# Four 32-row tiles for the samples' state update, rounded halves for the heads' sums, and another order of rows in the output projection

## The chip, the core and the metric

The kernel runs on one core of a Trainium2 chip. The metric is the device time of one execution in microseconds (us); less is better. The version before takes 2548.17 us, the median of three runs (2547.49 to 2548.25).

## What is computed

One decoder layer for 256 prompt tokens and 8 samples of 8 tokens, 320 tokens in all, with a model width of 2048. In the order of the reference:

```python
x = x + 0.5 * swiglu_ffn(rmsnorm(x, n_f1), f1_g, f1_u, f1_d)
m, s_new, buf_new = mixer(rmsnorm(x, n_mix), ...)        # w_in, heads and convolutions, w_out
x = x + m
x = x + cross_attn(rmsnorm(x, n_xa), mk, mv, xa_q, xa_o)
x = x + 0.5 * swiglu_ffn(rmsnorm(x, n_f2), f2_g, f2_u, f2_d)
y = rmsnorm_final(x)
```

The change lies in the mixer. One projection `w_in` feeds eight HGRN2 heads (group A) and a convolution of 31 taps over 1024 channels with a layer norm (group B); `w_out` maps their 2048 outputs back. A head keeps a 128 x 128 state per sequence. For each of the eight samples it computes

```python
S = exp(b_end)[..., None] * S + jnp.einsum('nhse,nhsd->nhed', k_to_end, vc)
o = rmsnorm(o, gnorm) * jax.nn.silu(zg)
```

with a sum over the sample's eight tokens in the first line (`k_to_end` is named `ket`, the tokens' values `vt`), and a mean over the head's 128 channels in the second.

## The kernel before

**Layout.** Activations lie with features on the 128 partitions and the 320 tokens along the free axis, so that the 2048 features are 16 tiles of 128 x 320. Weights come from memory in units of 128 x 1024 fp32 (eight blocks of 128 x 128). Each unit is split (lines 122 to 124) into a rounded high half `whi` in the type fp32r, cast by ScalarE (ACT), and the rest `wlo`, subtracted by VectorE (DVE). A block product (`mm3`, lines 188 to 195) is three fp32r matmuls into one PSUM bank: high by high, high by low, low by high. Matmuls on plain fp32 operands are used for the small products; the profile shows each of them as two instructions (transposes as one).

**PSUM.** Eight banks, in two sets of four: `acc` holds the sums of the projections, `sm` everything small.

**Mixer, input side.** `mixer_order` alternates convolutions and heads: c0, c1, h0, c2, h1, ... c7, h6, h7. A convolution takes two strips of `w_in` (16 blocks each), a head four (f, q, i, g in `head_in`). What follows a strip is not issued at once, but comes from two lists of generators: `hq` holds the heads' work (`head`, lines 639 to 764) and `cq` the convolutions' (`conv_taps`, 35 steps each, then `conv_norm`, 18 steps). After every fourth block product `pump` advances `hq` by one step and `cq` by CRATE = 1.65 steps on average. A step ends at a `yield`. So the order of the program interleaves projection and small work; within this order a scheduler places an instruction earlier or later when its operands are ready earlier or later.

**A head's steps.** Two empty ones; seven levels of a doubling scheme (lines 648 to 674, each a product of k and q into an `sm` bank, then DVE work on `qk` and a masked copy), with an empty step behind each, except in head 7; then transposes of k to tokens (`ket`) and of v (`vt`, `to_tokens`, lines 631 to 637: three transposes, one bank, one ACT copy); `vm`, eight copies of the last 64 tokens' values, each with the rows of one sample kept by the mask `vmask` (lines 687 and 688); the samples' read of the old state (line 695); the sums `po` (lines 707 and 710, a bank held to the head's end); the scaling of the eight states by ACT (line 717) and the prompt's chunk states (lines 723 to 730); the chunks' reads (line 710); the square `o2`; and then, in one step, lines 743 to 759:

```python
for b in range(2):                       # four samples each, 32 rows
    nc.tensor.matmul(ps, ket[rows, 2, :], vm[rows, 4 * b : 4 * b + 4, :]..., tile_position=(64 + 32 * b, 0))
    nc.vector.tensor_tensor(so, so, ps, ALU.add)
nc.tensor.matmul(ps[:, :T], ones, o2, start=True, stop=True)
root(o2, ps[:, :T], P)
```

`root` (lines 207 to 215) is square root, reciprocal and a correction step on ACT and DVE, with a scratch bank of `sm`. The last step scales, multiplies by the gate and splits the result into the pair `oc[h]`.

**Mixer, output side.** After the last strip, `while cq["jobs"]: pump()` empties the convolutions' list with no block products between. Then `w_out` is applied in two parts of 16 output tiles by 8 input tiles, part 0 with the convolutions' rows (8 to 15), part 1 with the heads' (0 to 7); `tick` goes on pumping, and `drain` empties both lists between the parts. Each output tile's sum lies in an `acc` bank until a DVE add to `x` (line 790).

Of the kernel before, what the change touches and what calls it, by code (L numbers as in the profile page):

```python
# [10 lines left out]
F32 = mybir.dt.float32  # L11
F32R = mybir.dt.float32r
U8 = mybir.dt.uint8
AF = mybir.ActivationFunctionType
ALU = mybir.AluOpType
AX = mybir.AxisListType

P = 128
DM = 2048
KT = DM // P  # L20
FF = 5632
FT = FF // P
NP = 256
NS = 64
T = NP + NS
# [26 lines left out]

CRATE = 1.65

# [7 lines left out]
def restride(ap, offset, dims):  # L62
    base = ap.ap
    return dataclasses.replace(ap, offset=ap.offset + offset, ap=[list(base[0])] + [list(d) for d in dims])


def hymba(tc, A, O):
# [3 lines left out]
    def tl(pool, shape, dt, tag, bufs):  # L71
        count[0] += 1
        return pool.tile(shape, dt, tag=tag, name=f"{tag}_{count[0]}", bufs=bufs)
# [9 lines left out]
    with (  # L83
# [11 lines left out]
        def sm():  # L95
            return tl(pp, [P, 512], F32, "sm", 4)
# [10 lines left out]
        msk = cp.tile([P, len(LEVELS), T], U8, name="msk")  # L107
        vmask = cp.tile([P, NSEQ], F32, name="vmask")
        sel = cp.tile([P, NS], F32, name="sel")
# [43 lines left out]
        def unit():  # L153
            while len(units) < 2 * G_TOT and len(units) < upos[0] + ahead[0]:
                fetch()
            u = units[upos[0]]
            units[upos[0]] = None
            upos[0] += 1
            return u
# [338 lines left out]
        with phase("mixer") as wk:  # L498

            def tmp(tag, bufs=2, w=T):  # L500
                return tl(wk, [P, w], F32, tag, bufs)

            qpad = wk.tile([P, NSEQ, 32], F32, name="qpad")
            nc.gpsimd.memset(qpad, 0.0)
            dws = [None] * NC
            csum = []
# [94 lines left out]
            def head_in(h):  # L601
                s0 = tl(wk, [P, NSEQ, P], F32, "t4", 4)
                nc.sync.dma_start(s0, A["s0"][h])
# [26 lines left out]

            def to_tokens(src, tag, bufs):
                ps = sm()
                for b, t0 in enumerate((0, P, T - P)):
                    nc.tensor.transpose(ps[:, b * P : (b + 1) * P], src[:, t0 : t0 + P], ident)
                out = tl(wk, [P, 3, P], F32, tag, bufs)
                nc.scalar.copy(out.rearrange("p a b -> p (a b)"), ps[:, : 3 * P])
                return out

            def head(h, s0, f, qk, late):
# [41 lines left out]
                )  # L681
                ket = to_tokens(k, "ket", 2)
                yield
                vt = to_tokens(late["v"], "vt", 2)
                up = slice(64, P)
                vm = tl(wk, [P, NSEQ, P], F32, "t4", 4)
                for i in range(NSEQ):
                    nc.scalar.activation(vm[up, i, :], vt[up, 2, :], AF.Copy, scale=vmask[up, i : i + 1])
                yield
# [50 lines left out]
                nc.scalar.activation(o2, po[:, :T], AF.Square)  # L740
                yield

                for b in range(2):
                    rows = slice(64 + 32 * b, 96 + 32 * b)
                    ps = sm()
                    nc.tensor.matmul(  # L746
                        ps,
                        ket[rows, 2, :],
                        vm[rows, 4 * b : 4 * b + 4, :].rearrange("p a b -> p (a b)"),
                        start=True,  # L750
                        stop=True,
                        tile_position=(64 + 32 * b, 0),
                    )
                    so = s0[:, 4 * b : 4 * b + 4, :].rearrange("p a b -> p (a b)")
                    nc.vector.tensor_tensor(so, so, ps, ALU.add)
                nc.sync.dma_start(O["ss"][h], s0)
                ps = sm()
                nc.tensor.matmul(ps[:, :T], ones, o2, start=True, stop=True)
                root(o2, ps[:, :T], P)
# [9 lines left out]
            for kind, i in mixer_order():  # L769
# [4 lines left out]
                else:  # L774
                    head_in(i)
            while cq["jobs"]:
                pump()


            stat = Stat(True)  # L780
            xg = []
            for part in range(2):
                if part:
                    drain()
                for n in range(KT):
                    ps = acc()
                    w = unit()
                    for kk in range(8):
                        mm3(ps[:, :T], w, kk, *oc[(1 - part) * NH + kk], kk == 0, kk == 7)
                    nc.vector.tensor_tensor(xs[n], ps[:, :T], xs[n], ALU.add)  # L790
                    if part:
                        xg.append(scaled_split(n, "xattn"))
                        stat.add(xs[n])
# [205 lines left out]
def pack(i):  # L999
# [9 lines left out]
    wout = strips(f["w_out"][0])  # L1009
    for half in (wout[:, :, 1024:], wout[:, :, :1024]):  # L1010
        groups.append(half.reshape(8, 2, P, 1024).transpose(0, 2, 1, 3).reshape(8, P, 2048))
    groups.append(strips(f["xattn_wq"][0]))
# [27 lines left out]
    for t0 in (0, P, NP):  # L1040
# [4 lines left out]
        for j, (H, wd) in enumerate(LEVELS):  # L1045
# [6 lines left out]
            msk[:, j, t0 : t0 + n] = m  # L1052
    vmask = np.zeros((P, NSEQ), np.float32)
    for j in range(NSEQ):
        vmask[64 + j * TS : 64 + (j + 1) * TS, j] = 1.0
    sel = np.zeros((P, NS), np.float32)
# [54 lines left out]
```

## Time and profile before

| | |
|---|---|
| median of three runs | 2548.17 us |
| the profiled execution's own time | 2546.1 us |
| its span, first to last instruction | 2544.3 us |
| TensorE clock granted | 0.998 of full speed |
| PE busy (matmuls) | 2521.4 us, 99% |
| DVE busy | 1482.4 us, 58% |
| ACT busy | 1047.3 us, 41% |
| DMA | 393.18 MB, mean 155 GB/s |

The profile is one execution. Engines: PE is TensorE's matmuls, PEld its weight loads, DVE is VectorE, ACT is ScalarE, POOL is GpSimd. L746 is line 746. In a timeline row stand the start in us from the span's start, the duration (of a run of rows: from the first start to the last end), engine, line, operation, the tiles written and read, and the count; what stands in brackets is how long the engine had been idle and what released it. Matmuls are pipelined, so that a row's duration is longer than the distance to the next row's start; it is the starts that tell the cost. The strips of `w_in` run from 984.9 to 1387.7 us, and part 0 of `w_out` follows.

### The profile page before, as it was taken

What the parts mean: (1) busy time and instruction counts of PE and PEld (TensorE: products, weight loads), DVE (VectorE), ACT (ScalarE), POOL (GpSimd) and SP (SyncE); (2) the same over time, 40 slices, a digit from 0 to 9 for tenths busy, and PEclk for the clock granted to TensorE, in tenths of its full rate; (3) what the DMA queues carried; (4) which work ended last, traced back from release to release, by engine and by line L of the source; (5) the groups of instructions that cost most, each with busy time, mean ns of one, the idle gap of its engine ahead of it and who ended that gap; (6) DMA issues with size and microseconds to landing.
All of it is one profiled execution on the core that took longest, in us unless ns stands there. A gap on an engine that the chain in (4) does not pass through costs nothing.

```text
span 2544.3 us, 41630 instructions
## 1 busy us (share of the span) xinstructions
PE 2521.4 (99%) x17300; PEld 2485.8 (98%) x17300; DVE 1482.4 (58%) x2115; ACT 1047.3 (41%) x1447; POOL 77.6 (3%) x88
## 2 busy tenths in 40 slices
PE   9999999999999999999999999999999999999997
PEld 9999999999999999999999999999999999999997
DVE  7555444444444567899888676644444444444444
ACT  6433333333333355555557455433333333333334
POOL 0100000000000020000000021100000000000002
PEclk9999999999999999999999999999999999999999
DMA  6544444444444446444443454444444444444443
GB/s 225 196 149 150 150 149 149 149 149 150 150 150 151 150 153 209 153 155 150 141 148 129 146 207 164 149 150 149 151 151 150 150 151 150 150 149 150 149 149 108
DMA packets 111357, 393.18 MB, mean 155 GB/s; under 512 B 12608, under 2 KB 16704, under 8 KB 111168
## 3 DMA queue, kind: packets, MB, share of 16 engines
q1 hardware_dynamic: 111024, 390.35, 45.5%
q8 instruction: 136, 2.23, 0.4%
q14 instruction: 53, 0.43, 0.0%
q10 hardware_dynamic: 144, 0.16, 0.0%
HBM read 380.71 MB, written 9.76 MB: 153 GB/s over the span
## 4 chain that ended last, share of the span: by engine, by line
PE 95%; DVE 2%; DMA 1%; ACT 1%; issue 1%; SPq 0%; POOLq 0%; DVEq 0%; ACTq 0%
PE acc L192 30%; PE acc L194 30%; PE acc L193 30%; PE sm L651 1%; DVE wlo L124 1%; PE acc L480 1%; PE acc L479 1%; PE acc L478 1%; DVE xgl L248 0%; PE sm L710 0%; ACT whi L123 0%; PE sm L746 0%; DMA t4k<-in_msk 0%; DMA mem<-in_mem 0%; DMA x<-in_x 0%
## 5 line engine op out<-in xcount | busy, mean ns | idle before, releaser
L123 ACT CAST whi<-raw 128x1024 fp32r<-128x1024 f32 (+1 forms) x692 | 722.2, 1045 | 1377.3 <-PE acc L193 981.5
L124 DVE TENSOR_TENSOR wlo<-raw,whi 128x1024 fp32r<-128x1024 f32 (+1 forms) x692 | 845.0, 1222 | 532.9 <-ACT whi L123 530.9
L192 PE MATMUL acc<-xgh,whi 128*128 128x320 f32 x3616 | 1128.4, 312 | 0.8 <-ACT whi L123 0.5
L194 PE MATMUL acc<-xgh,wlo 128*128 128x320 f32 x3616 | 1118.4, 309 | 1.0 <-DVE wlo L124 1.0
L193 PE MATMUL acc<-xgl,whi 128*128 128x320 f32 x3616 | 1117.7, 309 | 0.5 <-DVE xgl L248 0.4
L192 PEld LDWEIGHTS acc<-xgh,whi 128*128 128x128 f32 x3616 | 679.1, 188 | 4.6 <-issue 2.2
L193 PEld LDWEIGHTS acc<-xgl,whi 128*128 128x128 f32 x3616 | 679.1, 188 | 1.9 <-DVE xgl L248 1.0
L194 PEld LDWEIGHTS acc<-xgh,wlo 128*128 128x128 f32 x3616 | 678.7, 188 | 2.0 <-DVE wlo L124 1.7
L192 PE MATMUL acc<-hh,whi 128*128 128x320 f32 x1728 | 535.2, 310 | 2.1 <-ACT hh L123 2.0
L193 PE MATMUL acc<-hl,whi 128*128 128x320 f32 x1728 | 534.7, 310 | 1.5 <-DVE hl L124 1.5
L194 PE MATMUL acc<-hh,wlo 128*128 128x320 f32 x1728 | 534.1, 309 | 0.0
L192 PEld LDWEIGHTS acc<-hh,whi 128*128 128x128 f32 x1728 | 324.1, 188 | 4.2 <-ACT hh L123 2.8
L193 PEld LDWEIGHTS acc<-hl,whi 128*128 128x128 f32 x1728 | 324.4, 188 | 2.7 <-DVE hl L124 2.0
L194 PEld LDWEIGHTS acc<-hh,wlo 128*128 128x128 f32 x1728 | 324.4, 188 | 0.3 <-issue 0.2
L297 DVE SCALAR_TENSOR_TENSOR x<-acc,x 128x320 f32<-128x320 f32 x192 | 94.0, 490 | 228.2 <-PE acc L194 228.1
L230 POOL TENSOR_TENSOR ssq<-ssq,sq 128x320 f32<-128x320 f32 x57 | 62.1, 1089 | 1848.9 <-ACT sq L228 947.0
L550 DVE SCALAR_TENSOR_TENSOR hl<-u,vec,hl 128x256 f32<-128x256 f32 x240 | 112.3, 477 | 1.6
L262 DVE TENSOR_TENSOR fb<-acc,fa 128x320 f32<-128x320 f32 x87 | 42.7, 490 | 106.3 <-PE acc L194 106.2
L254 DVE TENSOR_TENSOR fa<-acc,r 128x320 f32<-128x320 f32 x87 | 42.7, 490 | 104.9 <-PE acc L194 104.9
L124 DVE TENSOR_TENSOR hl<-fb,hh 128x320 fp32r<-128x320 f32 x88 | 44.7, 509 | 0.0
L256 DVE TENSOR_TENSOR fa<-fa,r 128x320 f32<-128x320 f32 x88 | 42.5, 484 | 1.0 <-ACT fa L255 1.0
L255 ACT ACTIVATE fa<-fa 128x320 f32<-128x320 f32 x88 | 40.9, 465 | 4.2 <-DVE fa L254 4.2
(213 smaller groups left out, 1058.8 us busy)
## 6 DMA issues: line engine op xcount, KB each, us to landing
raw<-in_w SPq DMA_DIRECT2D x687, 512.0 KB, 3.6
t<-in_s SPq DMA_DIRECT2D x8, 512.0 KB, 5.0
out_ss<-t SPq DMA_DIRECT2D x8, 512.0 KB, 4.1
kv<-in_ck SPq DMA_DIRECT2D x8, 512.0 KB, 5.6
kv<-in_cv SPq DMA_DIRECT2D x8, 512.0 KB, 5.6
mem<-in_mem SPq DMA_DIRECT2D x4, 512.0 KB, 6.4
out_conv<-u SPq DMA_DIRECT2D x8, 167.0 KB, 3.5
x<-in_x SPq DMA_DIRECT2D x2, 640.0 KB, 7.3
```

Source lines behind the costliest of these rows:

```text
L123: nc.scalar.copy(hi, src)
L124: nc.vector.tensor_tensor(lo, src, hi.bitcast(F32), ALU.subtract)
L192: nc.tensor.matmul(out, hi, xh, start=first, stop=False)
L193: nc.tensor.matmul(out, hi, xl, start=False, stop=False)
L194: nc.tensor.matmul(out, lo, xh, start=False, stop=last)
L230: nc.gpsimd.tensor_tensor(self.total, self.total, s, ALU.add)
L254: nc.vector.tensor_tensor(t, pg[:, :T], r, ALU.mult)
L255: nc.scalar.activation(t, t, AF.Silu)
L256: nc.vector.tensor_tensor(t, t, r, ALU.mult)
L262: nc.vector.tensor_tensor(h, pu[:, :T], t, ALU.mult)
L297: nc.vector.scalar_tensor_tensor(xs[n], ps[:, :T], 0.5, xs[n], ALU.mult, ALU.add)
L550: nc.vector.scalar_tensor_tensor(dw[:, :NP], u[:, j : j + NP], cw, dw[:, :NP], ALU.mult, ALU.add)
```

## The change

Four edits.

1. The samples' state update. The sample tokens of k and v are spread so that each quarter of 32 partitions holds the 16 tokens of two samples (`spread` into the zeroed `kpad` and `vpad`, one ACT copy each). k's third transpose reads `kpad`; v gets a fourth transpose, of `vpad`. `vm` is then two full copies in place of eight half ones. The update is four products of 32 rows by 256 columns, at the tile positions (0, 0), (32, 0), (64, 0) and (96, 0), into four banks (three `sm`, one `acc`), followed by four DVE adds of 256 columns in place of two of 512.
2. The head's sum of squares. `o2` is split into two fp32r halves, `oh` (ACT) and `ol` (DVE), and summed by two fp32r matmuls with `ones_r` in place of one fp32 matmul. The sum and `root` move one step (one `yield`) behind the state update.
3. The order in `w_out`. Part 0 takes the rows of heads 0 to 6, part 1 the convolutions' and then head 7's; the weights are packed in memory to match, with the same bytes. Ahead of part 0 the loop now empties the heads' list down to its last entry, and the convolutions' list goes on in part 0.
4. CRATE is 1.5. The tag of `s0` and `vm` had four buffers; `s0` has three, `vm` one of its own.

```diff
--- before.py
+++ after.py
@@ -50,7 +50,10 @@
 
 G_TOT = 2 * 3 * FT + 8 + 48 + 16 + 4 + 4
 
-CRATE = 1.65
+CRATE = 1.5
+
+
+OUTPARTS = [list(range(7)), list(range(8, 16)) + [7]]
 
 
 def mixer_order():
@@ -105,7 +108,7 @@
         ident = cp.tile([P, P], F32, name="ident")
         eps = cp.tile([P, 1], F32, name="eps")
         msk = cp.tile([P, len(LEVELS), T], U8, name="msk")
-        vmask = cp.tile([P, NSEQ], F32, name="vmask")
+        vmask = cp.tile([P, 2], F32, name="vmask")
         sel = cp.tile([P, NS], F32, name="sel")
         at = [cp.tile([P, T], F32, name=f"at{i}") for i in range(2)]
         lb = cp.tile([P, NH], F32, name="lb")
@@ -500,8 +503,14 @@
             def tmp(tag, bufs=2, w=T):
                 return tl(wk, [P, w], F32, tag, bufs)
 
+            ones_r = wk.tile([P, P], F32R, name="ones_r")
+            nc.scalar.copy(ones_r, ones)
             qpad = wk.tile([P, NSEQ, 32], F32, name="qpad")
             nc.gpsimd.memset(qpad, 0.0)
+            kpad = wk.tile([P, P], F32, name="kpad")
+            nc.gpsimd.memset(kpad, 0.0)
+            vpad = wk.tile([P, P], F32, name="vpad")
+            nc.gpsimd.memset(vpad, 0.0)
             dws = [None] * NC
             csum = []
             oc = [None] * KT
@@ -599,7 +608,7 @@
                     yield
 
             def head_in(h):
-                s0 = tl(wk, [P, NSEQ, P], F32, "t4", 4)
+                s0 = tl(wk, [P, NSEQ, P], F32, "t4", 3)
                 nc.sync.dma_start(s0, A["s0"][h])
                 pf = acc()
                 strip(xg, pf[:, :T])
@@ -628,12 +637,17 @@
                 nc.scalar.activation(gt, pg[:, :T], AF.Silu)
                 late["g"] = gt
 
-            def to_tokens(src, tag, bufs):
+
+            def spread(dst, src):
+                nc.scalar.copy(restride(dst, 0, [[32, 4], [1, 16]]), restride(src, 0, [[16, 4], [1, 16]]))
+
+            def to_tokens(srcs, tag, bufs):
                 ps = sm()
-                for b, t0 in enumerate((0, P, T - P)):
-                    nc.tensor.transpose(ps[:, b * P : (b + 1) * P], src[:, t0 : t0 + P], ident)
-                out = tl(wk, [P, 3, P], F32, tag, bufs)
-                nc.scalar.copy(out.rearrange("p a b -> p (a b)"), ps[:, : 3 * P])
+                n = len(srcs)
+                for b, src in enumerate(srcs):
+                    nc.tensor.transpose(ps[:, b * P : (b + 1) * P], src, ident)
+                out = tl(wk, [P, n, P], F32, tag, bufs)
+                nc.scalar.copy(out.rearrange("p a b -> p (a b)"), ps[:, : n * P])
                 return out
 
             def head(h, s0, f, qk, late):
@@ -679,13 +693,15 @@
                     restride(qpad.rearrange("p a b -> p (a b)"), 0, [[64, 4], [40, 2], [1, TS]]),
                     restride(q, NP, [[2 * TS, 4], [TS, 2], [1, TS]]),
                 )
-                ket = to_tokens(k, "ket", 2)
-                yield
-                vt = to_tokens(late["v"], "vt", 2)
-                up = slice(64, P)
-                vm = tl(wk, [P, NSEQ, P], F32, "t4", 4)
-                for i in range(NSEQ):
-                    nc.scalar.activation(vm[up, i, :], vt[up, 2, :], AF.Copy, scale=vmask[up, i : i + 1])
+                spread(kpad, k[:, NP:])
+                ket = to_tokens((k[:, :P], k[:, P:NP], kpad), "ket", 2)
+                yield
+                v = late["v"]
+                spread(vpad, v[:, NP:])
+                vt = to_tokens((v[:, :P], v[:, P:NP], v[:, T - P :], vpad), "vt", 2)
+                vm = tl(wk, [P, 2, P], F32, "vm", 1)
+                for i in range(2):
+                    nc.scalar.activation(vm[:, i, :], vt[:, 3, :], AF.Copy, scale=vmask[:, i : i + 1])
                 yield
                 px = sm()
                 for i2 in range(2):
@@ -739,23 +755,28 @@
                 o2 = tmp("vT")
                 nc.scalar.activation(o2, po[:, :T], AF.Square)
                 yield
-
-                for b in range(2):
-                    rows = slice(64 + 32 * b, 96 + 32 * b)
-                    ps = sm()
+                oh, ol = tl(wk, [P, T], F32R, "oh", 1), tl(wk, [P, T], F32R, "ol", 1)
+                split(oh, ol, o2)
+
+                pn = [sm()[:, : 2 * P], sm()[:, : 2 * P], sm()[:, : 2 * P], acc()[:, : 2 * P]]
+                for c in range(4):
+                    rows = slice(32 * c, 32 * c + 32)
                     nc.tensor.matmul(
-                        ps,
+                        pn[c],
                         ket[rows, 2, :],
-                        vm[rows, 4 * b : 4 * b + 4, :].rearrange("p a b -> p (a b)"),
+                        vm[rows].rearrange("p a b -> p (a b)"),
                         start=True,
                         stop=True,
-                        tile_position=(64 + 32 * b, 0),
+                        tile_position=(32 * c, 0),
                     )
-                    so = s0[:, 4 * b : 4 * b + 4, :].rearrange("p a b -> p (a b)")
-                    nc.vector.tensor_tensor(so, so, ps, ALU.add)
+                for c in range(4):
+                    so = s0[:, 2 * c : 2 * c + 2, :].rearrange("p a b -> p (a b)")
+                    nc.vector.tensor_tensor(so, so, pn[c], ALU.add)
                 nc.sync.dma_start(O["ss"][h], s0)
+                yield
                 ps = sm()
-                nc.tensor.matmul(ps[:, :T], ones, o2, start=True, stop=True)
+                nc.tensor.matmul(ps[:, :T], ones_r, oh, start=True, stop=False)
+                nc.tensor.matmul(ps[:, :T], ones_r, ol, start=False, stop=True)
                 root(o2, ps[:, :T], P)
                 yield
                 nc.vector.tensor_tensor(o2, po[:, :T], o2, ALU.mult)
@@ -773,20 +794,22 @@
                         cq["jobs"].append(conv_norm())
                 else:
                     head_in(i)
-            while cq["jobs"]:
+            while len(hq["jobs"]) > 1:
                 pump()
-
 
             stat = Stat(True)
             xg = []
-            for part in range(2):
+            i = 0
+            for part, tiles in enumerate(OUTPARTS):
                 if part:
                     drain()
                 for n in range(KT):
                     ps = acc()
-                    w = unit()
-                    for kk in range(8):
-                        mm3(ps[:, :T], w, kk, *oc[(1 - part) * NH + kk], kk == 0, kk == 7)
+                    for kt in tiles:
+                        if i % 8 == 0:
+                            w = unit()
+                        mm3(ps[:, :T], w, i % 8, *oc[kt], kt == tiles[0], kt == tiles[-1])
+                        i += 1
                     nc.vector.tensor_tensor(xs[n], ps[:, :T], xs[n], ALU.add)
                     if part:
                         xg.append(scaled_split(n, "xattn"))
@@ -1007,8 +1030,10 @@
         cols = (32 + j, 40 + j) if kind == "c" else (8 + j, j, 16 + j, 24 + j)
         groups += [win[c : c + 1] for c in cols]
     wout = strips(f["w_out"][0])
-    for half in (wout[:, :, 1024:], wout[:, :, :1024]):
-        groups.append(half.reshape(8, 2, P, 1024).transpose(0, 2, 1, 3).reshape(8, P, 2048))
+    wout = wout.reshape(KT, P, KT, P)
+    for tiles in OUTPARTS:
+        a = wout[:, :, tiles, :].transpose(1, 0, 2, 3).reshape(P, -1, 2048)
+        groups.append(a.transpose(1, 0, 2))
     groups.append(strips(f["xattn_wq"][0]))
     wo = strips(f["xattn_wo"][0])
     groups.append(wo.reshape(4, 4, P, 512).transpose(0, 2, 1, 3).reshape(4, P, 2048))
@@ -1050,9 +1075,10 @@
             else:
                 m = (s // (2 * H) == t // (2 * H)) & (s % (2 * H) < H) & (t % (2 * H) >= H)
             msk[:, j, t0 : t0 + n] = m
-    vmask = np.zeros((P, NSEQ), np.float32)
-    for j in range(NSEQ):
-        vmask[64 + j * TS : 64 + (j + 1) * TS, j] = 1.0
+    vmask = np.zeros((P, 2), np.float32)
+    for j in range(2):
+        for c in range(4):
+            vmask[32 * c + j * TS : 32 * c + (j + 1) * TS, j] = 1.0
     sel = np.zeros((P, NS), np.float32)
     for j in range(NS):
         sel[j // 16 * 32 + j % 16, j] = 1.0
```

## The prediction

> **What bounds the kernel now.** I read the page first, then busy time by stage, then what PE waited for in the mixer.
>
> ```profile
> span 2544.3 us, 41630 instructions
> PE 2521.4 (99%) x17300; PEld 2485.8 (98%) x17300; DVE 1482.4 (58%) x2115; ACT 1047.3 (41%) x1447; POOL 77.6 (3%) x88
> ```
>
> ```profile
> core 0: us, PE busy (x) PEld busy (x) DVE busy (x) ACT busy (x) POOL busy (x), PEclk, DMA share, GB/s
> 100.00:940.00 840.00, 839.03 (x5718) 838.49 (x5717) 418.38 (x517) 291.77 (x348) 15.73 (x13) 1.00 0.44 150
> 1030.00:1360.00 330.00, 329.92 (x2372) 318.67 (x2371) 290.68 (x565) 183.92 (x305) 0.62 (x5) 1.00 0.45 149
> 1380.00:1400.00 20.00, 17.36 (x134) 16.19 (x133) 14.42 (x26) 17.03 (x36) 0.00 (x0) 1.00 0.26 88
> ...
> 2520.00:2545.00 25.00, 8.93 (x55) 7.70 (x53) 11.49 (x15) 6.82 (x14) 4.19 (x5) 0.78 0.28 106
> ```
>
> ```profile
> PE acc L192 <- ACT hh L123: 2.0, 1, 2.0
> PE acc L193 <- DVE hl L124: 0.6, 1, 0.6
> ```
>
> The reader is to see that PE has work all the time. The first window gives the price of a projection matmul in a dense stretch: 840 us for 5718, 0.147 us each. Through the heads (second window) PE is never idle, DVE is busy for 88% and ACT for 56%. So there a matmul saved is time saved, and what DVE and ACT do is hidden as long as it comes in time. The one hole in the mixer is in the third window, and the waits name it: PE waits for the rounded high halves `hh` of the convolutions, then for the low ones.
>
> ```profile
> 1387.57 0.31 PE L194 MATMUL acc<-xgh,wlo 128*128 128x320 f32 x1
> 1387.72 0.49 PE L634 MATMUL sm<-ident,vT 128*128 128x128 f32 x3
> 1388.14 0.65 PE L695 MATMUL sm<-t,qpad 128*32 128x128 f32 x16
> 1390.83 0.70 PE L192 MATMUL acc<-hh,whi 128*128 128x320 f32 x3 [2.04 <-ACT hh L123]
> 1392.13 0.41 PE L193 MATMUL acc<-hl,whi 128*128 128x320 f32 x1 [0.60 <-DVE hl L124]
> ```
>
> This is the end of the last strip. Three matmuls need 0.44 us, so those from 1390.83 end at 1391.27 and the next begins at 1392.13: 0.86 lost. L695 needs 0.57 (below), to 1388.71: 2.12 lost. The hole is 3.0 us.
>
> **The change, part by part.** Prices on PE come from the chain of waits, where each piece is the time until the next one starts:
>
> ```profile
> 948.57 0.54 PE sm L237 x2
> ...
> 1326.84 0.44 PE sm L651 x4
> ...
> 1332.90 0.33 PE sm L634 x3
> ...
> 1334.98 0.57 PE sm L695 x16
> ...
> 1337.51 0.22 PE sm L707 x2
> 1337.73 0.62 PE sm L710 x6
> ...
> 1340.17 0.65 PE sm L723 x8
> 1340.82 0.34 PE acc L192
> ...
> 1344.53 0.61 PE sm L710 x6
> ...
> 1348.72 1.06 PE sm L746 x4
> 1349.78 0.74 PE sm L758 x2
> ```
>
> ```profile
> L746 PE MATMUL sm<-t,ket x4: 587/640/692, 1348.6 to 1349.2; 32*128 32x512 f32 x4
> ```
>
> *State update.* An fp32 product costs 0.54 us for 320 columns (L237), 1.69 ns a column; 512 columns are 0.86. The two row tiles of L746 together take 1.06, not 1.73: they run side by side, with 0.20 around them. Four tiles of 256 columns, all side by side, are 0.43 + 0.20 = 0.63: 0.43 less per head. The trace has no four row tiles; the bounds are this and two after two, 0.86 + 0.20, no gain. I take the first: L695 runs 16 instructions, four column tiles at a time, in 0.57, where 8 products of 128 columns in a row would need 1.73. The Trainium skill (TensorE: Matmul & The Clock Gate, Part 3, Measured speedup vs the span model) has four row tiles at 3.07 times one by one, not 4; by that the four would take an estimated 1.73 / 3.07 = 0.56 in place of 0.43, and the gain over seven heads would be 0.9 us smaller. The pair in L746 loses nothing to its neighbour beyond the 0.20 that is counted, so the sum goes by the row.
>
> *Sum of squares.* L758 costs 0.74: 0.54 for 320 columns and 0.20 for coming back from the row tiles. The second stays, behind the update (after L723's tiles L192 likewise shows 0.34 instead of 0.15). Two fp32r matmuls cost 2 x 0.147 = 0.29. Saved: 0.25.
>
> *The fourth transpose.* L634 gives 0.33 for three: 0.11 more.
>
> Per head PE gains 0.43 + 0.25 - 0.11 = 0.57 us.
>
> *Beside PE.*
>
> ```profile
> L124 DVE TENSOR_TENSOR wlo<-raw,whi 128x1024 fp32r<-128x1024 f32 x99 | 120.6, 1219 | 25.3 <-ACT whi L123 24.4
> L212 DVE RECIPROCAL vT<-vT 128x320 f32<-128x320 f32 x8 | 17.2, 2146 | 0.4 <-ACT vT L210 0.4
> L755 DVE TENSOR_TENSOR t<-t,sm 128x512 f32<-128x512 f32 x16 | 10.6, 682 | 2.7 <-PE sm L746 1.7 <-PE acc L192 1.0
> L660 DVE TENSOR_TENSOR qk<-qk,fall 128x256 f32<-128x256 f32 x24 | 10.1, 420 | 7.2 <-PE sm L651 7.2
> L730 DVE SCALAR_TENSOR_TENSOR st<-st,fall,sm 128x128 f32<-128x128 f32 x24 | 8.2, 343 | 0.3
> L575 DVE TENSOR_TENSOR hl<-hl,mu 128x320 f32<-128x320 f32 x8 | 3.6, 485 | 0.0
> ```
>
> ```profile
> L717 ACT ACTIVATE t<-t,fall 128x128 f32<-128x128 f32 x64 | 20.6, 391 | 0.1
> L688 ACT ACTIVATE t<-vt,vmask 64x128 f32<-64x128 f32 x64 | 19.8, 385 | 0.3
> L210 ACT ACT_TABLE_LOAD x8 | 10.3, 1283 | 0.1
> ```
>
> DVE gets the subtraction for `ol`, a pass like L575 (0.49), and four adds of 256 columns (0.42, L660) for two of 512 (0.68): 0.8 us more per head, 6.5 in all, into the 39 us in which it is idle in the second window. ACT loses eight copies of L688 (2.5 us) and gets about 1.7: two full copies, the cast, two spreads. Both at nothing; without that cover they would cost the heads what they measure. The new wait is the sum's for `ol`. Behind it on PE stand the strips' matmuls, and who waits for it is the head's own end. The `yield` puts 12 strip matmuls (1.76 us) ahead of it, against 0.95 for cast and subtraction, so I count nothing; L758 now shows one of 0.21 (row below), and that in head 6 alone. SP's queue keeps its transfers, with the same bytes; the store of the states stays behind the adds, and no other moved step issues one. A cast of `ones` and two memsets on POOL, once, lie ahead of the first head. Nothing for these.
>
> *The order in `w_out`.* The old hole goes, since part 0 no longer needs the convolutions: 3.0 us. What is late next is head 6. Counting the steps: `hq` moves one step per 4 blocks, 24 per pair of head and convolution, and a head takes 26 of them now, 25 before (its last is shared with the next head's first). So `hq` falls two steps behind with each head instead of one, and after the last strip head 6 still owes its levels 5 and 6 and all that follows. Before, it was at its px step (L695). The new loop issues these 15 pumps with no projection between them, and every output tile of part 0 needs head 6 for its seventh block.
>
> How long does head 6 take from there? On the bare path: two levels 2 x (0.44 + 0.42), spread 0.25 (half a pass), transposes 0.33, copy 0.49, L723 0.65, states 4 x 0.34, reads 0.61, square, cast and subtraction 3 x 0.49 (a pass of 128x320 is taken as L575's) make 6.9 us. From the sum of squares on: 0.46 (two matmuls 0.15 apart, 0.31 long), square root 0.49, reciprocal 2.15, six more passes of 0.49 make 6.0. The second half can be seen in the trace, for the same head:
>
> ```profile
> 1406.61 0.81 PE L758 MATMUL sm<-vT,ones 128*128 128x320 f32 x2 [0.21 <-ACT vT L740]
> ```
>
> ```profile
> 1417.08 0.48 DVE L124 TENSOR_TENSOR hl<-vT,hh 128x320 fp32r<-128x320 f32 x1
> ```
>
> It took 10.95 us, 1.8 times the bare path, since weight splits, adds and other work stand between. With that factor the 12.9 us become 23.
>
> What can PE do in 23 us? It need not stand: the timeline shows projection matmuls of part 0 moved ahead as soon as their tiles are ready (three L192 in a row above). Heads 0 to 5 are ready, so four output tiles can be begun, one per `acc` bank: 4 x 6 x 3 x 0.147 = 10.6 us. Head 6's own products, from the rows: 0.88 + 0.33 + 0.44 + 0.57 + 0.84 + 0.65 + 0.61 + 0.63 + 0.29, and 0.6 for coming back from tiles: 5.8. The convolutions' two sums: 1.1. Head 7's first levels are ready as well; I allow three, 1.5. Together 19. The new hole is 23 - 19 = 4 us.
>
> *Sum.* Seven heads gain 0.57 each, 4.0 (head 6 pays into the hole, where PE isn't the bound); the old hole 3.0; the new one costs 4. Change: -3.0 us on the profiled execution's 2546.1, and the same on the median of 2548.17, which is 2.1 above it: 2545.2 us.
>
> **Rivals.**
>
> *No new hole.* If the scheduler keeps head 6 close to the bare path (12.9 us and some waiting) or lets more of head 7 in, PE has 19 us of work against 13 to 19 and never stands: -7.0, 2541.2 us. For it: PE had no hole in head 6's second half in the old part 0. Against it: DVE and ACT then had less to do.
>
> *Head 6 queues behind the convolutions (slower).* With CRATE 1.5 the convolutions' norm is issued in the same 15 pumps. It is four passes of eight (L575's 3.6 us each, 14.4), a root (3.2) and four weight splits of 1.22, beside head 6's own 9 us: 31 us of DVE work. ACT meanwhile has the states' eight scalings (2.6), squares, silus and table loads of 1.28. If all of that stands ahead of head 6's end, it comes after 31 us and the hole is 12 at the least. The banks add to it: `po` holds one of the four `sm` banks, the update takes the other three, and the sum and the root's scratch need two more, so both wait for the DVE adds; and if the update's fourth product takes an `acc` bank, only three output tiles fill the time, 2.6 less: a hole of 15, change +8, 2556 us. It decides from a hole of 12. For it: DVE at 88%, and the hole before had just this cause, late halves behind ACT. Against it: head 6's steps precede the convolutions' in each pump. The Trainium skill (TensorEngine Tiling (Array Packing), Gotcha 1: PSUM Pressure) warns of this, that row tiles write to different banks and row tiling raises the pressure on them; the rows here show only that L755 follows L746.
>
> *Clock.* In the last window, where PE is mostly idle, the granted clock is 0.78. If a hole in one piece did that here, at most 25 x 0.22 = 5.5 us would be lost: up to +2.5, 2550.7 us. Against it: 1.00 across the 3.0 us hole. The Trainium skill (TensorE: Matmul & The Clock Gate, Part 1) has the clock halved after an idle window of about 3.4 us; the hole above is too short to test it.
>
> *It doesn't do what it says.* The four tiles run two by two: PE gains 0.14 per head, change 0, 2548.2 us.
>
> **How the numbers follow.** Forecast (hole of 2 to 12): 0.57. No hole to 2 us: 0.24. Queue: 0.12. Clock: 0.04. Two by two: 0.03. A change of 0.2%, 5.1 us, is about what a measurement can tell from none. Faster by more needs a hole under 2, or four tiles and a little luck: 0.26. Slower by more is the queue: 0.12. Between: 0.62. The range goes from -7.5 (no hole, and some more) to +4 (a hole of 11): 2540.7 to 2552.2. Left out are most of the queue and what I haven't thought of.
>
> **What would show it.** Right: the update's eight instructions within 0.7 us, the sum's two at 0.15; the strips ending 5 to 6 us earlier (six heads at 0.57, and what of head 6 moves behind them); then projection matmuls on `hh` at once, with no wait for the convolutions, and PE idle about 4 us in all before the first matmul on head 6's tile, released by ACT or DVE. Wrong: strips of the same length, holes within them at the sums or for an `acc` bank, waits of part 1 for convolutions or head 7, or a hole far from 4.

## The result, and the profile after

The changed kernel takes 2552.83 us (median of 13 runs, 2551.95 to 2553.48) against 2547.85 us for the kernel before (13 runs, 2544.71 to 2549.45): 1.0019 times as long, interval 1.0012 to 1.0026. The prediction was 2545.2, with a range that ended at 2552.2. So the kernel is slower by about 0.2%, and the forecast of -3.0 us was wrong by 8.

The page after, its span and its engines:

```profile
span 2551.1 us, 41698 instructions
PE 2521.1 (99%) x17340; PEld 2489.2 (98%) x17340; DVE 1483.1 (58%) x2139; ACT 1037.0 (41%) x1422; POOL 77.7 (3%) x90
```

PE shows the same busy time as before in a span that is 6.8 us longer. Where the time lies is read from the starts of the matmuls: the strips of `w_in` from the first to the last, and `w_out` from the end of the last strip to its own end.

| us | strips | `w_out` | both | after that |
|---|---|---|---|---|
| before | 402.8 | 131.2 | 534.0 | 1025.4 |
| after | 396.6 | 143.0 | 539.7 | 1025.3 |

The strips are 6.2 us shorter, `w_out` is 11.8 longer: +5.7. The other 1.1 us of the two spans lie ahead of the mixer. That stretch differs by up to 3.0 us between the profiled executions of all the kernels below, so profiles are compared by the table's third column from here on.

*The heads pay as forecast.* The same level of two successive heads in the chain of waits, before and after:

```profile
1033.44 0.45 PE sm L651 x4
...
1087.11 0.44 PE sm L651 x4
```

```profile
1034.59 0.45 PE sm L665 x4
...
1089.47 0.44 PE sm L665 x4
```

A head's period was 53.67 us; now it is 54.88. It has one step more, that is 4 block products of 3 matmuls of 0.147 us, 1.76; without these it is 53.12, 0.55 less. Predicted were 0.57.

*What comes behind the strips.* PE's waits after (total, count, longest), and the windows from the last strip's end at 1382.69 on:

```profile
PE sm L665 <- DVE qk L669: 6.2, 1, 6.2
```

```profile
core 0: us, PE busy (x) PEld busy (x) DVE busy (x) ACT busy (x) POOL busy (x), PEclk, DMA share, GB/s
1382.69:1390.26 7.57, 5.87 (x53) 4.15 (x51) 6.88 (x17) 6.01 (x16) 0.00 (x0) 1.00 0.39 126
1390.26:1404.80 14.54, 14.54 (x95) 13.24 (x94) 10.90 (x22) 8.98 (x20) 0.00 (x0) 1.00 0.07 24
1404.80:1411.00 6.20, 0.05 (x1) 0.02 (x1) 5.67 (x13) 6.20 (x15) 0.00 (x0) 0.68 0.11 43
1411.00:1418.00 7.00, 6.05 (x26) 5.88 (x27) 5.71 (x13) 4.03 (x7) 0.00 (x0) 0.55 0.00 0
```

PE is idle for 1.7, then for 6.15, then for 0.95 us; and in the last 7 us the granted clock is 0.55, which is worth up to 7 x 0.45 = 3.2 us. That makes 12.0. The table says the same: the heads' 3.9 (seven times 0.55) and the old hole's 3.0 should have left 534.0 - 6.9 = 527.1, and it is 539.7: the new hole costs 12.6 us, where 4 were forecast. The old wait for `hh` is gone.

The hole in PE's timeline:

```profile
1382.69 0.61 PE L665 MATMUL sm<-qk 128*128 128x128 f32 x4
...
1389.64 0.69 PE L764 MATMUL acc<-vm,ket 32*128 32x256 f32 x2
1390.26 0.41 PE L195 MATMUL acc<-hh,whi 128*128 128x320 f32 x1
...
1399.44 0.70 PE L764 MATMUL sm<-vm,ket 32*128 32x256 f32 x4
...
1400.86 0.69 PE L764 MATMUL sm<-vm,ket 32*128 32x256 f32 x2
...
1401.48 0.41 PE L778 MATMUL sm<-oh,ones_r 128*128 128x320 f32 x1
...
1403.93 0.31 PE L197 MATMUL acc<-hh,wlo 128*128 128x320 f32 x1
...
1411.01 1.19 PE L665 MATMUL sm<-qk 128*128 128x128 f32 x4 [6.16 <-DVE qk L669]
```

Part 0 is begun from 1390.26 to 1404.07, with 72 matmuls on heads 0 to 5, just as many as were counted. Then PE has nothing left. Head 6 meanwhile, on DVE and on ACT:

```profile
1394.49 0.49 DVE L127 TENSOR_TENSOR ol<-vT,oh 128x320 fp32r<-128x320 f32 x1 [0.95 <-ACT oh L126]
...
1403.58 2.15 DVE L215 RECIPROCAL vT<-vT 128x320 f32<-128x320 f32 x1
...
1410.38 0.48 DVE L669 TENSOR_TENSOR qk<-qk,f 128x320 f32<-128x320 f32 x1
...
1413.62 0.53 DVE L127 TENSOR_TENSOR hl<-vT,hh 128x320 fp32r<-128x320 f32 x1
```

```profile
1398.52 0.44 ACT L216 ACTIVATE sm<-mu 128x320 f32<-128x320 f32 x1 [1.80 <-DVE mu L215]
...
1402.14 0.53 ACT L213 ACTIVATE vT<-sm,eps 128x320 f32<-128x320 f32 x1 [3.18 <-PE sm L779]
1402.68 1.28 ACT L599 ACT_TABLE_LOAD   x1
1403.98 1.20 ACT L599 ACTIVATE hl<-hl,vec 128x320 f32<-128x320 f32 x2
...
1408.16 0.51 ACT L214 ACTIVATE sq<-sm,eps 128x320 f32<-128x320 f32 x1
```

These rows are read in three steps. The operands of the sum, `oh` and `ol`, are ready at 1394.98, 12.3 us behind the last strip. But the sum (L778) starts at 1401.48, since the update's remaining tiles (L764) come only at 1399.44 and 1400.86. Just ahead of them, at 1398.52, the convolutions' `root` first writes its scratch bank (L216 writes `sm`). Then head 6's own `root` stops between its square root (1402.14) and its second ACT pass (L214, 1408.16), though that pass reads the same bank as the square root, and the reciprocal (L215) ends at 1405.73: a table load and the convolutions' silus (L599) with their casts stand between. Head 6's low half ends at 1414.15, 31.5 us after the last strip. The projection goes on at once with it.

### The profile page after: what moved, and what is told of

Its sections match the earlier page's. It is cut to its first block, busy times and chain, and to the rows that moved or that the text cites. A ratio compares the mean times of both kernels' runs of the same rounds, so it can differ in the third digit from the quotient of the medians.

```text
span 2551.1 us, 41698 instructions
## 1 busy us (share of the span) xinstructions
PE 2521.1 (99%) x17340; PEld 2489.2 (98%) x17340; DVE 1483.1 (58%) x2139; ACT 1037.0 (41%) x1422; POOL 77.7 (3%) x90
## 4 chain that ended last, share of the span: by engine, by line
PE 95%; DVE 2%; DMA 1%; issue 1%; ACT 1%; SPq 0%; POOLq 0%; DVEq 0%; ACTq 0%
PE acc L195 30%; PE acc L197 30%; PE acc L196 30%; PE sm L665 1%; DVE wlo L127 1%; PE acc L483 1%; PE acc L482 1%; PE acc L481 1%; DMA x<-in_x 1%; DVE xgl L251 0%; PE sm L726 0%; DMA t4k<-in_msk 0%; PE sm L648 0%; DMA mem<-in_mem 0%; DVE x L966 0%
## 5 line engine op out<-in xcount | busy, mean ns | idle before, releaser
L126 ACT CAST whi<-raw 128x1024 fp32r<-128x1024 f32 (+1 forms) x692 | 722.3, 1045 | 1370.8 <-PE acc L196 962.4
L665 PE MATMUL sm<-qk 128*128 128x128 f32 x224 | 35.6, 282 | 7.8 <-DVE qk L669 6.2
```

Of the source, the lines that this page charges most:

```text
L126: nc.scalar.copy(hi, src)
L665: nc.tensor.matmul(g[:, s], k[:, s], q[:, s], start=True, stop=True)
```

## The experiments

Theory A: head 6 is late because the convolutions' norm, issued in the same 15 pumps, takes its banks and stands ahead of it on ACT and DVE. Theory B, the rival: head 6 takes this long from its own steps, since too much of it is left behind the strips. They part where the convolutions' work is taken out of these pumps, and where head 6 is brought forward. The expectations, written before each run, call A "theory C" and B "L"; W, in conv_scratch, says that the work on DVE and ACT sets head 6's end, whatever the banks. In all kernels that follow, the kernel before is at 2547.1 to 2548.0 us (10 to 33 runs); ratios are to it.

**heads_alone.** The loop ahead of part 0 empties the heads' list only; the convolutions' list goes on in part 0.

```diff
-        def pump():
-            for q in queues:
+        def pump(some=None):
+            for q in some or queues:
...
-                pump()
+                pump([hq])
```

> The changed kernel, but the loop ahead of part 0 advances the heads' list only; the convolutions' norm is left to the pumps of part 0. Theory C (the convolutions' norm, issued in the same 15 pumps, holds head 6 up: its root's scratch bank stands ahead of the update's banks in the shared set, and its silus stand ahead of head 6's root on ACT): head 6's low half is ready about 20 us after the last strip instead of 31, PE stands 4 us instead of 13, and the clock stays at 1.00; about 2544 us. Rival L (head 6 simply has too many steps behind the last strip, whoever else works): ready at 28 us or later, hole 10 or more; 2550 us or above.

Measured: 2544.55 us (2543.1 to 2547.85), 0.9991 [0.9982, 0.9999]: 8.3 us less than the change. The profiled execution's PE timeline has its last strip's end at 1383.63 and the sum of squares at

```profile
1394.45 0.47 PE L778 MATMUL sm<-oh,ones_r 128*128 128x320 f32 x1
```

and three of its windows are

```profile
1384.00:1392.00 8.00, 6.42 (x54) 4.65 (x52) 3.93 (x10) 5.16 (x15) 0.00 (x0) 1.00 0.27 97
1392.00:1393.00 1.00, 1.00 (x6) 0.74 (x6) 0.42 (x1) 0.30 (x1) 0.00 (x0) 0.68 0.22 66
1393.00:1399.00 6.00, 6.00 (x24) 5.35 (x23) 3.31 (x4) 3.09 (x7) 0.00 (x0) 0.50 0.23 90
```

The sum comes 10.8 us after the last strip instead of 18.8, and head 6's low half (a DVE row at 1406.19, 0.48 long) ends after 23.0 us instead of 31.5. So by the medians 8.3 of the 12.6 us go with the convolutions in the same pumps, and 4.3 are left for theory B and the clock. The profiled execution is the slowest of its eleven, 3.3 us above their median; in it 533.8 - 527.1 = 6.7 us of the hole are left by the strips and `w_out`, and up to half of the 6.8 us at clock 0.50 (from about 1392.3 to 1399.1) is in that.

**conv_scratch.** The convolutions' `root` takes its scratch from SBUF instead of an `sm` bank.

```diff
-        def root(r, ps, n):
+        def root(r, ps, n, a=None):
             v = tl(mp, [P, r.shape[-1]], F32, "sq", 2)
-            a = sm()[:, : r.shape[-1]]
+            a = sm()[:, : r.shape[-1]] if a is None else a
...
-                root(rs, ps[:, :T], NC * P)
+                root(rs, ps[:, :T], NC * P, tmp("sg", 1))
```

> The changed kernel, but the scratch of the convolutions' root lies in SBUF instead of a bank of the shared set. Theory C, bank part: the update's products start by 11 us after the last strip instead of 17, the sum's matmuls at about 13 instead of 19, and the hole shrinks by 3 to 6 us, to 2547 to 2550 us; the rest stays, since the silus still stand ahead on ACT. Rival W (the sum of the work on DVE and ACT sets head 6's end, whatever the banks): the sum moves earlier, but head 6's low half stays at 31 us; no change, 2553 us.

Measured: 2550.11 us (2548.62 to 2551.71), 1.001 [1.0001, 1.0019], 2.7 less than the change. PE and ACT, where the last strip ends at 1380.65:

```profile
1393.13 0.70 PE L764 MATMUL sm<-vm,ket 32*128 32x256 f32 x4
...
1394.96 0.41 PE L778 MATMUL sm<-oh,ones_r 128*128 128x320 f32 x1
...
1407.46 0.68 PE L665 MATMUL sm<-qk 128*128 128x128 f32 x4 [4.53 <-ACT hl L599]
```

```profile
1406.79 1.20 ACT L599 ACTIVATE hl<-hl,vec 128x320 f32<-128x320 f32 x2
...
1408.23 0.45 ACT L126 CAST hh<-vT 128x320 fp32r<-128x320 f32 x1
```

The update's remaining tiles begin 12.5 us after the last strip instead of 16.8, and the sum 14.3 instead of 18.8. So the bank is shown: 4.5 us earlier. But 2.5 of these are lost again: head 6's low half (a DVE row at 1409.62, 0.48 long) ends after 29.5 us instead of 31.5, as head 6's last cast (L126 from `vT`) now stands behind four pairs of silus on ACT. Banks and queue are both at work, and taking one away moves the wait to the other.

**old_order.** Edits 1 and 2 alone, with the convolutions first, the old loop and CRATE 1.65.

```diff
-CRATE = 1.5
+CRATE = 1.65
-OUTPARTS = [list(range(7)), list(range(8, 16)) + [7]]
+OUTPARTS = [list(range(8, 16)), list(range(8))]
...
-            while len(hq["jobs"]) > 1:
+            while cq["jobs"]:
```

> The new state update and sum of squares with the old order of w_out, the old loop and a rate of 1.65. If the heads gain what the trace of the changed kernel seems to show (0.56 us of PE each, hidden nowhere): 8 x 0.56 = 4.5 us below before, 2543.4 us, with the old hole of 3 us back behind the last strip. If the gain is lost again (one more step per head, banks held by the update): within 1 us of before, 2547 to 2548 us.

Measured: 2546.95 us (2544.59 to 2548.36), 0.9997 [0.9988, 1.0006]. The strips are as short as in the change (396.9) and `w_out` takes 137.2, 6 more than before: the heads' gain is given back whole. A wait and a window:

```profile
PE sm L665 <- DVE qk L674: 4.3, 1, 4.3
```

```profile
1388.00:1394.00 6.00, 5.24 (x21) 4.94 (x22) 5.89 (x17) 5.99 (x14) 0.00 (x0) 0.50 0.10 38
```

So the new steps bring a hole of their own with the old order too: head 6, which now still owes its last two levels, waits for DVE, PE stands for 4.3 us, and the clock is 0.50 for the next 6. By the strips and `w_out` the holes here come to 534.1 - 527.1 = 7.0 us, and to 12.6 with the new order. So the order of `w_out` isn't the root of it, but it makes it larger.

**heads_faster.** The change as it is, with the heads' list 12% faster: 24 x 1.12 = 26.9 steps per pair of head and convolution, where a head has 26.

```diff
-            hq = {"rate": 1, "jobs": []}
+            hq = {"rate": 1.12, "jobs": []}
```

> The changed kernel with a rate of 1.12 instead of 1 for the heads' list, so that it keeps up with 26 steps per 24 pumps and head 6 is through its steps about when the last strip ends. Theories C and L alike: almost nothing of head 6 is left to wait for, the hole is 0 to 4 us and the clock stays at 1.00; 2540 to 2544 us. If the hole comes from the new order itself (weights run out while their buffers wait for head 6, or DVE lags behind): hole above 8 us again, 2549 us or above.

Measured: 2540.61 us (2539.31 to 2541.23), 0.9972 [0.9961, 0.9982]: 12.2 less than the change, 7.2 less than before. This is the best version. Strips 402.9 and `w_out` 125.2, together 528.1, beside the 527.1 worked out above for no hole. The windows over the place of the hole, and the one wait of a new step:

```profile
1380.00:1400.00 20.00, 20.00 (x144) 19.04 (x143) 13.67 (x24) 10.45 (x17) 0.00 (x0) 1.00 0.32 110
1400.00:1420.00 20.00, 20.00 (x152) 19.17 (x151) 17.89 (x34) 14.23 (x31) 0.00 (x0) 1.00 0.42 142
```

```profile
PE sm L778 <- DVE t L774: 0.6, 1, 0.6
```

PE never stands and the clock is full. Head 6 is through before the convolutions' norm begins, so that both causes fall away together.

**old_order_faster.** Is the new order still worth something when the heads keep up? `old_order` with the faster list.

```diff
-            hq = {"rate": 1, "jobs": []}
+            hq = {"rate": 1.12, "jobs": []}
```

> New state update and sum, old order of w_out, rate 1.12 for the heads' list, so that head 6 is through when the last strip ends. If the run with the old order lost its gain to head 6's late levels and to the clock behind the last strip: the gain of 8 x 0.56 = 4.5 us shows, 2543 us, with the old hole of 3 us or less. If the heads' gain is not there at all: 2547 us.

Measured: 2544.95 us (2543.94 to 2548.89), 0.9991 [0.9982, 1.0]. It is 4.3 above heads_faster, 3.8 by the strips and `w_out` (531.9). PE's waits show the old hole again, 1.1 us for the high halves and the longer of the two waits for low ones, 1.2 (the other lies outside the mixer, in heads_faster too):

```profile
PE acc L196 <- DVE hl L127: 2.1, 2, 1.2
...
PE acc L195 <- ACT hh L126: 1.1, 1, 1.1
```

**faster_old_sum.** heads_faster with the old fp32 sum of squares (`oh`, `ol` and `ones_r` gone, the added `yield` kept).

```diff
...
-                split(oh, ol, o2)
...
-                nc.tensor.matmul(ps[:, :T], ones_r, oh, start=True, stop=False)
-                nc.tensor.matmul(ps[:, :T], ones_r, ol, start=False, stop=True)
+                nc.tensor.matmul(ps[:, :T], ones, o2, start=True, stop=True)
```

> As the run with the rate of 1.12 (2540.6 us), but with the head's sum as one fp32 matmul again; the step structure stays. By the rows the two fp32r matmuls save 0.24 us of PE per head, so 8 x 0.24 = 1.9 us more: 2542.5 us. If the fp32r pair saves nothing on the path: 2540.6 us.

Measured: 2542.38 us (2540.81 to 2544.57), 0.998 [0.9971, 0.9988], 1.8 above heads_faster: 0.22 for each of eight heads, where 0.25 was the price. The ranges overlap by 0.4 us; in the profiled executions, this kernel's being the slowest of its runs, the strips are 1.4 longer, 0.20 for each of seven heads, and `w_out` 1.8.

**new_order_faster.** The other way round: the new order, loop and CRATE, rate 1.12, and the heads of before (edits 1 and 2 undone).

```diff
...
-                pn = [sm()[:, : 2 * P], sm()[:, : 2 * P], sm()[:, : 2 * P], acc()[:, : 2 * P]]
-                for c in range(4):
+                for b in range(2):
...
-                nc.tensor.matmul(ps[:, :T], ones_r, oh, start=True, stop=False)
-                nc.tensor.matmul(ps[:, :T], ones_r, ol, start=False, stop=True)
+                nc.tensor.matmul(ps[:, :T], ones, o2, start=True, stop=True)
...
-            hq = {"rate": 1, "jobs": []}
+            hq = {"rate": 1.12, "jobs": []}
```

> The kernel before with only the new order of w_out, the new loop, CRATE 1.5, and a rate of 1.12 for the heads' list; state update, transposes and sum as before. It should lie 8 x 0.56 = 4.5 us above the run with all edits at that rate (2540.6): 2545.1 us, which is the old hole of 3 us below before. If the order's gain is more than its hole (the clock falls in some executions of before): 2543 us. If the order gains nothing: 2547.8 us.

Measured: 2547.97 us (2546.16 to 2549.48), 1.0 [0.9991, 1.0009]. This missed. `w_out` has no hole (125.0 us), but the strips take 409.5, and both together are 6.4 more than in heads_faster, where 4.5 were expected. PE's waits account for 1.5 of it:

```profile
PE sm L713 <- ACT xi L707: 1.5, 7, 0.3
```

That is a wait of 0.2 us in each of seven heads for a copy, which before, after and heads_faster don't show. The last 0.4 us remain open. Neither the new order alone at a rate of 1 nor the raised rate alone was run, so what each gives by itself isn't known.

**no_yield.** The change without the `yield` that it puts between update and sum; a head has 25 steps again, and head 6 should owe as little as before.

```diff
                 nc.sync.dma_start(O["ss"][h], s0)
-                yield
                 ps = sm()
```

> The changed kernel without the one added yield: the sum of squares and the root stand in the step of the state update again, 25 steps per head as before. Theory C+L (the added step makes head 6 owe 15 pumps behind the last strip instead of 8, and these 15 reach the convolutions' root and silus, which 8 do not): the hole is 1 to 4 us, no clock loss; 2541 to 2545 us. Rival (the hole belongs to the new order, one step more or less does not matter, or PE now waits for the low half in every head): 2549 us or above.

Measured: 2551.25 us (2549.65 to 2554.07), 1.0014 [1.0005, 1.0023]. This missed too: the time is the rival's, though not by what the rival names. Head 6's low half does come earlier, 19 us after the last strip. But there are two waits that weren't expected, and the second goes by DVE's queue:

```profile
PE sm L777 <- DVE t L774: 4.1, 7, 0.6
PE acc L195 <- DVE x L812: 4.0, 2, 3.7
```

```profile
1405.18 2.15 DVE L215 RECIPROCAL mu<-mu 128x320 f32<-128x320 f32 x1 [0.29 <-ACT mu L213]
1407.25 3.43 DVE L127 TENSOR_TENSOR wlo<-raw,whi 128x1024 fp32r<-128x1024 f32 x3
1410.60 0.48 DVE L812 TENSOR_TENSOR x<-acc,x 128x320 f32<-128x320 f32 x1
```

Directly behind the update, the sum needs a bank that the adds (L774) have yet to free: 0.6 us per head. And when head 6 is ready, the four begun output tiles end at once, their adds (L812) stand behind the convolutions' reciprocal and three weight splits, and no `acc` bank is free meanwhile. Behind this wait of 3.7 us the clock is again 0.50, from about 1412.3 to 1415.6. The `yield` that lengthens the head is needed; its rate has to pay for it.

**six_heads.** What if part 0 did not need head 6 at all? Part 0 takes the rows of heads 0 to 5, part 1 the convolutions' and those of heads 6 and 7; there is no loop ahead of part 0.

```diff
-OUTPARTS = [list(range(7)), list(range(8, 16)) + [7]]
+OUTPARTS = [list(range(6)), list(range(8, 16)) + [6, 7]]
...
-            while len(hq["jobs"]) > 1:
-                pump()
```

> The changed kernel at rate 1, but part 0 of w_out takes heads 0 to 5 only, part 1 the convolutions, then heads 6 and 7; no loop ahead of part 0, since these six heads are through. Theory L (the hole is there because every output tile of part 0 needs the head that the list still owes): no hole and full clock behind the last strip. What is left unfilled is ten pumps of head 7 between the parts, with 8 ready tiles for each of four banks to fill 14 us: hole 0 to 4 there, 2541 to 2545 us. Rival (the hole only moves: head 7's end between the parts costs as much as head 6's did, with the clock): 2548 us or above.

Measured: 2556.04 us (2553.5 to 2556.53), 1.003 [1.0017, 1.0042]. The hole behind the strips is gone, the first projection matmul follows at once. But the last ten steps of head 7, which shared part 0's end with projection matmuls in the change, are now issued between the parts, and no projection matmul stands beside head 7 from 1434.1 to 1456.8, though the convolutions' last low half was ready at 1437.2. So the hole has moved, as the rival said. One of its levels, and the windows there:

```profile
1441.55 1.22 PE L665 MATMUL sm<-qk 128*128 128x128 f32 x4 [0.52 <-DVE qk L674]
```

```profile
1434.00:1436.00 2.00, 1.11 (x8) 0.74 (x6) 2.00 (x5) 1.77 (x3) 0.00 (x0) 1.00 0.64 219
1436.00:1438.00 2.00, 0.31 (x1) 0.31 (x2) 2.00 (x6) 0.00 (x0) 0.00 (x0) 0.71 0.20 57
...
1446.00:1448.00 2.00, 2.00 (x21) 1.25 (x20) 0.00 (x0) 1.62 (x5) 0.00 (x0) 0.50 0.00 0
...
1460.00:1462.00 2.00, 2.00 (x13) 2.00 (x12) 1.79 (x1) 0.03 (x1) 1.21 (x5) 0.82 0.17 61
```

The clock falls at about 1437 and is back only at about 1460.7. The four instructions of the level took 0.61 us at full clock (1382.69 in the change).

**heads_alone_again.** The kernel of heads_alone once more, to see what its slow clock is worth.

> One more look at the kernel whose loop advances the heads' list only. Its first profiled execution was the slowest of its eleven, with the clock at 0.50 from about 1392.7 to 1399.5 us behind the last strip. Theory G (the clock halves for about 6.8 us after a thin stretch, in some executions and not in others, and costs 3.4 us): in an execution with the clock at 1.00 there, the stretch from the last strip to the end of w_out is 2.5 to 3.5 us shorter than 137.1. Rival (the stretch is slow for another reason): 136.5 to 137.5 whatever the clock.

Measured: 2543.35 us, one run. The clock fell here as well, but for a shorter time. The same window in the first execution and in this one:

```profile
1390.00:1400.00 10.00, 10.00 (x42) 8.38 (x43) 5.56 (x10) 4.70 (x11) 0.00 (x0) 0.66 0.16 61
```

```profile
1390.00:1400.00 10.00, 10.00 (x63) 9.52 (x60) 5.95 (x11) 3.20 (x7) 0.00 (x0) 0.84 0.14 54
```

The mean clock is 0.66 and 0.84, and `w_out` takes 137.1 and 135.6 us: 1.5 us for 10 x 0.18 = 1.8. The stretch at half clock is 6.8 us long in the first and 3.4 in this one. So by this one pair it costs a little under half its length. An execution with the clock at 1.00 throughout was not seen, so the rest of the price isn't measured.

## Why the prediction was wrong

*Right.* The state update and the sum of squares on PE: 0.57 a head was forecast, 0.55 measured, and the sum's 0.25 was 0.22 by itself. The four tiles run side by side, so the rival of two by two falls. The strips are 6.2 us shorter (an end 5 to 6 earlier was forecast). The old wait for `hh` is gone, and PE's fill is 72 matmuls from four `acc` banks, as counted. That head 6 would owe 15 pumps was right too.

*The step that failed* is "The new hole is 23 - 19 = 4 us": it is 12.6.

First, the 23. It was made from the bare path of 12.9 us times 1.8, a factor taken from the old part 0, where head 6 shared the engines with weight splits and adds but not with the convolutions' norm. In heads_alone, where the norm is out of these pumps, it is 23.0 us, and 21.6 in the second execution; in both the clock was low for some us, which the factor doesn't have, so the close match is in part luck. With the norm in the same pumps it is 31.5. This was the rival "head 6 queues behind the convolutions", which gave 31 us, a hole of 12 and more, and the banks as part of the cause; I gave it 0.12, with the argument that head 6's steps come first in each pump. They do within a pump, but counted through the lists the convolutions' `root` is issued three pumps ahead of the update, and its scratch bank keeps the update's last three tiles waiting, and the sum behind them (4.5 us, conv_scratch). And on ACT the silus stand ahead of passes of head 6's `root` (from 1402.14 to 1408.16). The Trainium skill (TensorEngine Tiling (Array Packing), Gotcha 1: PSUM Pressure) was cited for this rival; the traces agree, with the update's last tile 11.2 us behind its first in the change, and 6.8 in conv_scratch, where one bank more is free.

Second, the 19. As a size it was near: PE is busy for 5.87 + 14.54 = 20.4 us before it stands. But the work was counted as if it ran from the first moment. The scheduler put no projection matmul between head 6's steps from 1382.69 to 1390.26, so 1.7 us were lost there. Why none was placed there was not tried.

Third, the clock. I gave it 0.04 as a rival of its own, and it came on top of the queue: 0.55 over the 7 us behind the idle 6.15 us, up to 3.2 us. The row used against it, 1.00 across a hole of 3.0 us, says nothing of one twice as long. The Trainium skill (TensorE: Matmul & The Clock Gate, Part 1) names an idle window of about 3.4 us; the idle stretches of 6.16 us here, 4.33 in old_order, 4.53 in conv_scratch and 3.74 in no_yield are longer, and each has the clock at 0.50 behind it. That so long a stretch is needed they don't bear out: here the clock falls at about 1407.1, 2.2 us into the stretch, and in six_heads at about 1436.9, 1.4 us into one of 2.25.

*What was missed altogether*: the list's rate. The working found that the list falls two steps behind per head instead of one, and took the debt as given. Edits 1 and 2 alone already lose their gain to it (old_order), and 12% on the rate takes the hole away and makes the change a gain of 7.2 us (heads_faster), close to the -7.0 that the rival "no new hole" gave.

## What to carry to other kernels

Where small work is fed in at a fixed rate beside dense work, a step more per item is paid at the end, behind the last cover: raise the rate with the step, and read what the last item still owes. When a late stage is costed by a factor from the trace, ask what shares its engines and its banks in the new place; a factor taken from another neighbourhood didn't carry over here. And the cover lost cost twice here, once as idle time and again as clock.

## What the runs showed of the hardware

The granted clock halved without a long idle stretch. In heads_alone PE was busy with small products for 6.42 of 8 us, no idle piece being over 0.96 us and none lying behind 1386.42, and the clock was 0.50 from about 1392.3 to 1399.1. The Trainium skill (TensorE: Matmul & The Clock Gate, Part 1, A second HAM failure mode: psum-queue depth-cycling) tells of a clock that swings when PE idles briefly and often between groups. In heads_alone there are two such pieces (0.52 and 0.96 us), and the last ends 5.9 us before the clock falls, so this trace doesn't show that cause.

Nor did a busy PE bring it back. In six_heads PE's records lie without a gap from 1446 on, transposes at first and then small fp32 products, many of them on a part of the rows or columns, and the clock stayed at 0.50. The projection matmuls begin at 1456.8, and the clock rises at about 1460.7, 3.9 us later. Whether the small products' type or their tiles keep it down was not tried.

Four products of 32 rows, at four row positions, run side by side in full: in heads_faster the update takes 0.65 us from its first instruction (1385.33) to the next one's start (1385.98), where 0.63 was worked out from two tiles.

```profile
1385.33 0.49 PE L764 MATMUL sm<-vm,ket 32*128 32x256 f32 x3
...
1385.98 0.41 PE L195 MATMUL acc<-xgh,whi 128*128 128x320 f32 x1
```
